# LoRA linear layer on one NeuronCore: a second buffer of rounded rows, a load cut in two, and another wait before the first store

## The chip, the cores and the metric

The kernel runs on one core of one Trainium2 chip. The metric is device time in microseconds (us); the median of three runs of the kernel before is 164.86 us (164.70 to 165.10). A core has a matrix engine (TensorE, PE in the profile; its weight loads are listed as PEld), VectorE (DVE), ScalarE (ACT), GpSimd (POOL) and SyncE (SP), which here only issues transfers. The engines run side by side and meet at semaphores. Data moves between HBM and on-chip memory (SBUF) through 16 DMA engines; matrix results are written to PSUM, from which DVE or ACT copy them out.

## The reference

```python
x: [16, 2048, 256] f32     W: [256, 256] f32
lora_A: [256, 16]   lora_B: [16, 256]   lora_E: [16]   scale: 1.0

x_flat = x.reshape(-1, 256)                     # 32768 rows
y = x_flat @ W
lora_out = ((x_flat @ lora_A) * lora_E) @ lora_B
return (y + scale * lora_out).reshape(16, 2048, 256)
```

x is 33.6 MB and the output is as large, both float32. The kernel folds the low-rank part into one matrix, weff = W + scale * A diag(E) B, in bfloat16, and then computes x_flat @ weff.

## The kernel before

**Rows and chunks.** The 32768 rows are cut into eight chunks, numbered 0 to 7. `PLAN` (line 10) gives their sizes in rows per partition: 16, 32, 48, 48, 16, 16, 48, 32, which makes 256 on each of 128 partitions. A chunk of 16 is a transfer of 2 MB, one of 48 is 6 MB. In SBUF a ring `xy` of 176 rows per partition holds both the rows loaded and, written over them, the results. Chunks 0 to 5 fill the ring exactly, so chunks 6 and 7 are loaded into places whose results have been stored before.

**SP's order** is written out by hand and sets the order of the one DMA queue. SP issues W, load 0, the three small loads (lines 122 to 124) and loads 1 to 5 (line 126) without a wait. Then, for each chunk, it waits until the chunk's results are in the ring (`s_rdy`, line 128) and issues its store (line 132). Two more waits stand in this loop: before the first store SP waits until load `LEAD - 2` = 4 has landed (line 131), and after store 2 (`AFTER`, line 15) it waits for stores 0 and 1, issues load 6, waits for store 2, and issues load 7 (lines 133 to 136).

**A group** is 16 rows of each partition (`G`); there are 16 groups. For each group:

- DVE rounds the rows to bfloat16 in one instruction, into the one buffer `xb` (line 177, a CAST in the profile). At a chunk's first group it waits for the chunk's load first; at chunk 4 (`PAUSE`) it also waits until store 2 has landed (line 175).
- PE transposes the 16 rows in two parts of eight (line 200, into `ps_xt`, two bfloat16 values travelling as one float32 word), and DVE copies each part to SBUF (`xt`, line 191).
- PE multiplies (line 208, 32 matmuls into `ps_y`, four rows at a time, two buffers), and ACT copies each four rows back to the ring (line 157). The last `LATE` = 6 of these 64 copies are made by DVE, after its last copy of transposes.

DVE executes its instructions strictly in the order of the program: cast of group g, the two copies of g, cast of g+1, and so on. PE runs a hardware loop over the 16 groups (line 227), waiting for `xb`, for `xt` and for a free `ps_y`. POOL passes a chunk's last `ps_y` buffer back to PE (line 164).

**Start-up.** weff is made once: PE transposes A (it waits for A's own semaphore, line 216), DVE multiplies by E (waits for E's), POOL rounds B (waits for B's), PE multiplies, DVE adds W.

The core's last wait is for stores 3 to 7 (line 237; the profile gives it the number 268).

Of the kernel before, what the change touches and what calls it, by code (L numbers as in the profile page):

```python
# [6 lines left out]

PLAN = [16, 32, 48, 48, 16, 16, 48, 32]  # L10

RING = 176

LEAD = 6
AFTER = {2: [6, 7]}

PAUSE = 4

G, S, Q = 16, 8, 4

LATE = 6


@with_exitstack
def kernel(
# [11 lines left out]
    P = 128  # L37
    FP32 = mybir.dt.float32
    BF16 = mybir.dt.bfloat16

    x_flat = x.flatten_outer_dims()
    out_flat = out.flatten_outer_dims()
    N, K = x_flat.shape
    M = out_flat.shape[1]
    R = lora_B.shape[0]
    KC = K // P
    CHUNKS = len(PLAN)
    assert K == M == KC * P and sum(PLAN) * P == N and all(b % G == 0 for b in PLAN)

    def sbuf(name, shape, dt):  # L50
        return ctx.enter_context(nc.sbuf_tensor(name, shape, dt))

    def psum(name, shape, dt):
        return ctx.enter_context(nc.psum_tensor(name, shape, dt))

    xy = sbuf("xy", [P, RING, K], FP32)
    xb = sbuf("xb", [P, G, K], BF16)

    xt = [sbuf(f"xt{s}", [P, S, P, KC], BF16) for s in range(2)]
    w_sb = sbuf("w_sb", [P, KC, M], FP32)  # L60
    a_sb = sbuf("a_sb", [P, KC, R], FP32)
    b_sb = sbuf("b_sb", [R, M], FP32)
    e_sb = sbuf("e_sb", [R, 1], FP32)
    b_bf = sbuf("b_bf", [R, M], BF16)
    ate = sbuf("ate", [R, KC, P], BF16)
    weff = sbuf("weff", [P, KC, M], BF16)
    ident = sbuf("ident", [P, P], FP32)

    ps_xt = [psum(f"ps_xt{s}", [P, S, P], FP32) for s in range(2)]
    ps_y = [psum(f"ps_y{s}", [P, Q, M], FP32) for s in range(2)]  # L70

    ps_at = ps_y[0][:R, 0, :].rearrange("r (c p) -> r c p", c=KC)
    ps_aeb = ps_y[1][:, :KC, :]

    sem = tc.alloc_semaphore
    s_w, s_a, s_b, s_e = sem("s_w"), sem("s_a"), sem("s_b"), sem("s_e")
    s_in = [sem(f"s_in{i}") for i in range(CHUNKS)]
    starts = [sum(PLAN[:i]) for i in range(CHUNKS)]
    places = [r % RING for r in starts]
    assert sum(PLAN[:LEAD]) <= RING and all(r + b <= RING for r, b in zip(places, PLAN))  # L80

    owners = {
        i: [j for j in range(LEAD) if places[j] < places[i] + PLAN[i] and places[i] < places[j] + PLAN[j]]
        for i in range(LEAD, CHUNKS)
# [5 lines left out]
    s_lora = sem("s_lora")  # L90
    s_lpe = sem("s_lpe")
    s_xb = sem("s_xb")
    s_t = sem("s_t")
    s_xt = sem("s_xt")
# [4 lines left out]
    def rows_of(flat, i):  # L99
        b, r0 = PLAN[i], starts[i] * P  # L100
        return flat[r0:r0 + b * P, :].rearrange("(p b) k -> p b k", b=b)

    def ring_of(i):
        return xy[:, places[i]:places[i] + PLAN[i], :]


    def pieces(rows):
        return [(i, r) for i, b in enumerate(PLAN) for r in range(0, b, rows)]

    def rows_at(i, r, rows):  # L110
        return xy[:, places[i] + r:places[i] + r + rows, :]

    with tc.tile_critical(sync_engine=mybir.EngineType.SP, no_gpsimd_drain=True):  # L113
        sp, pe, dve, act, pool = nc.sync, nc.tensor, nc.vector, nc.scalar, nc.gpsimd


        def load(i):
            sp.dma_start(out=ring_of(i), in_=rows_of(x_flat, i)).then_inc(s_in[i], 16)

        sp.dma_start(out=w_sb[:], in_=W.rearrange("(p c) m -> p c m", c=KC)).then_inc(s_w, 16)  # L120
        load(0)
        sp.dma_start(out=a_sb[:], in_=lora_A.rearrange("(p c) r -> p c r", c=KC)).then_inc(s_a, 16)
        sp.dma_start(out=b_sb[:], in_=lora_B).then_inc(s_b, 16)
        sp.dma_start(out=e_sb[:], in_=lora_E[:, None]).then_inc(s_e, 16)
        for i in range(1, LEAD):
            load(i)
        for i in range(CHUNKS):
            sp.wait_ge(s_rdy, i + 1)
            if i == 0:

                sp.wait_ge(s_in[LEAD - 2], 16)
            sp.dma_start(out=rows_of(out_flat, i), in_=ring_of(i)).then_inc(s_out[min(i, again)], 16)
            for later in AFTER.get(i, []):
                for j in owners[later]:
                    sp.wait_ge(s_out[j], 16)
                load(later)
        for i in range(len(s_out) - 1):
            sp.wait_ge(s_out[i], 16)


        pool.memset(ident[:], 0.0).then_inc(s_id, 1)  # L141
        pool.wait_ge(s_id, 1)
        pool.affine_select(  # L143
            out=ident[:], in_=ident[:], compare_op=mybir.AluOpType.not_equal, fill=1.0,
            base=0, pattern=[[-1, P]], channel_multiplier=1,
        ).then_inc(s_id, 1)
        pool.wait_ge(s_b, 16)
        pool.tensor_copy(out=b_bf[:], in_=b_sb[:]).then_inc(s_lora, 1)  # L148

        copies = pieces(Q)

        def y_of(q, engine, copy):
            i, r = copies[q]
            engine.wait_ge(s_p, q + 1)
            done = copy(out=rows_at(i, r, Q), in_=ps_y[q % 2][:])  # L157
            if r + Q == PLAN[i]:
                done.then_inc(s_rdy, 1)
            else:  # L160
                done.then_inc(s_y[q % 2], 1)

        for i in range(CHUNKS - 1):
            pool.wait_ge(s_rdy, i + 1).then_inc(s_y[((starts[i] + PLAN[i]) // Q - 1) % 2], 1)


        for q in range(len(copies) - LATE):
            y_of(q, act, act.copy)


        for g, (i, r) in enumerate(pieces(G)):
            if r == 0:
                dve.wait_ge(s_in[i], 16)
            if r == 0 and i == PAUSE:
                dve.wait_ge(s_out[again - 1], 16)

            dve.tensor_copy(out=xb[:], in_=rows_at(i, r, G)).then_inc(s_xb, 1)  # L177
            if g == 0:
                dve.wait_ge(s_e, 16)
                dve.wait_ge(s_lpe, 1)  # L180
                dve.tensor_scalar(  # L181
                    out=ate[:], in0=ps_at, scalar1=e_sb[:], scalar2=float(scale),
                    op0=mybir.AluOpType.mult, op1=mybir.AluOpType.mult,
                ).then_inc(s_lora, 1)
                dve.wait_ge(s_w, 16)
                dve.wait_ge(s_lpe, 2)
                dve.tensor_add(out=weff[:], in0=w_sb[:], in1=ps_aeb).then_inc(s_lora, 1)  # L187
            for k in range(g * G // S, (g + 1) * G // S):

                dve.wait_ge(s_t, k + 1)  # L190
                dve.tensor_copy(  # L191
                    out=xt[k % 2][:].rearrange("w j p c -> w j (p c)"), in_=ps_xt[k % 2][:].bitcast(BF16),
                ).then_inc(s_xt, 1)
        for q in range(len(copies) - LATE, len(copies)):
            y_of(q, dve, dve.tensor_copy)


        def transposes(k):
            for j in range(S):
                t = pe.transpose(ps_xt[k % 2][:, j, :], xb[:, k * S + j, :].bitcast(FP32), ident[:])  # L200
            t.then_inc(s_t, 1)

        def products(k):
            for h in range(S // Q):
                pe.wait_ge(s_y[h], 1).then_inc(s_y[h], -1)  # L205
                for j in range(Q):
                    for c in range(KC):
                        m = pe.matmul(  # L208
                            ps_y[h][:, j, :], xt[k % 2][:, h * Q + j, :, c], weff[:, c, :],
                            start=(c == 0), stop=(c == KC - 1),  # L210
                        )
                m.then_inc(s_p, 1)

        for h in range(2):
            pe.sem_inc(s_y[h], 1)
        pe.wait_ge(s_a, 16)
        pe.wait_ge(s_id, 2)
        for c in range(KC):
            t = pe.transpose(ps_at[:, c, :], a_sb[:, c, :], ident[:])  # L219
        t.then_inc(s_lpe, 1)  # L220
        pe.wait_ge(s_lora, 2)
        for c in range(KC):
            m = pe.matmul(ps_aeb[:, c, :], ate[:, c, :], b_bf[:], start=True, stop=True)  # L223
        m.then_inc(s_lpe, 1)

        pe.wait_ge(s_lora, 3)
        with pe.Fori(0, sum(PLAN) // G):
            pe.wait_ge(s_xb, 1).then_inc(s_xb, -1)  # L228
            for k in range(G // S):
                transposes(k)  # L230
            for k in range(G // S):
                pe.wait_ge(s_xt, 1).then_inc(s_xt, -1)
                products(k)


    with tc.tile_critical(sync_engine=mybir.EngineType.SP, no_gpsimd_drain=True):
# [36 lines left out]
```

## Time and profile before

| | |
|---|---|
| median of the runs | 164.86 us |
| the profiled execution, its own time | 165.35 us |
| its span in the profile | 163.6 us |
| moved by the DMA engines | 67.4 MB, 412 GB/s over the span |
| PE busy | 96.8 us (59%) |
| DVE busy | 81.7 us (50%) |
| ACT busy | 57.2 us (35%) |
| cast of a group on DVE (line 177) | 16 of 2287 ns |
| copy of eight transposed rows on DVE (line 191) | 32 of 1220 ns |
| copy of four result rows on ACT (line 157) | 58 of 1016 ns |
| first store issued | 53.03 us |
| store 2 landed, load 7 issued | 88.4 us |
| last store issued | 143.66 us |

Times inside the span count from its start. A transfer's landing is the time of its issue plus the time to landing that the profile gives for the issue. Because there is one queue, transfers follow each other, and the difference of two successive landings is what the later one took of the queue. In the rows for stretches of time, each engine's busy time comes with the number of its instructions, then the clock that PE was granted (1.00 is full speed), the mean busy share of the 16 DMA engines, and the rate. A packet is counted where it starts, so rates of short stretches scatter. The value behind "idle before" or in square brackets is how long an engine stood before an instruction, and what ended that.

### The profile page before, as it was taken

To read this page: it belongs to the slowest core of one execution; us is meant where nothing else is said; L and a number is where in the kernel's file an instruction comes from. 1 tells how busy PE (TensorE), PEld (TensorE's weight loads), DVE (VectorE), ACT (ScalarE), POOL (GpSimd) and SP (SyncE) were. 2 spreads that over 40 slices of the span, in tenths; PEclk is the share of its full clock that TensorE was granted. 3 is DMA by queue.
4 is the path that set the end of the run, shared out by engine and by line. 5 is a ranking of instruction groups with operands and counts; after the bars stand their busy time and mean duration, and the time that the engine had idled before them with its cause. 6 is when DMAs were issued, how large, how long until landed. Compare 5 with 4: busy or idle time off the path is not lost. (4 is left out here: it accounts for less than half of the span.)

```text
span 163.6 us, 1911 instructions
## 1 busy us (share of the span) xinstructions
PE 96.8 (59%) x772; PEld 79.3 (49%) x772; DVE 81.7 (50%) x56; ACT 57.2 (35%) x59; POOL 2.9 (2%) x7
## 2 busy tenths in 40 slices
PE   0027989877888978984000788878889775700000
PEld 0006677756777757763000767667777564500000
DVE  0063767559486494650003485594864949710000
ACT  3000357472664844747000054926648400000000
POOL 1050000000000000000000000000000000000000
PEclk9999999999999999999755599999999998775555
DMA  5999988998899999999999997999997999989990
GB/s 152 433 440 457 513 385 385 445 517 385 385 405 437 377 433 465 409 425 529 421 397 385 409 517 341 441 457 401 469 469 337 429 429 481 505 385 397 425 409 16
DMA packets 2658, 67.42 MB, mean 412 GB/s; under 512 B 464, under 2 KB 480, under 8 KB 608
## 3 DMA queue, kind: packets, MB, share of 16 engines
q1 hardware_dynamic: 2656, 67.41, 96.8%
q14 instruction: 2, 0.02, 0.0%
HBM read 33.85 MB, written 33.55 MB: 412 GB/s over the span
## 5 line engine op out<-in xcount | busy, mean ns | idle before, releaser
L157 ACT COPY xy<-ps_y 128x1024 f32<-128x1024 f32 x58 | 56.0, 1016 | 72.8 <-PE ps_y L208 72.8
L208 PE MATMUL ps_y<-weff,xt 128*128 128x256 bf16 x512 | 64.0, 278 | 16.9 <-PEq L205 16.8
L208 PEld LDWEIGHTS ps_y<-weff,xt 128*128 128x128 bf16 x512 | 48.0, 100 | 32.2 <-issue 24.4
L191 DVE COPY xt<-ps_xt 128x2048 bf16<-128x2048 bf16 x32 | 37.9, 1220 | 31.4 <-PE ps_xt L200 31.3
L177 DVE CAST xb<-xy 128x4096 bf16<-128x4096 f32 x16 | 36.6, 2287 | 28.6 <-DMA out_dram<-xy 16.0
L200 PE MATMUL ps_xt<-ident,xb 128*128 128x128 f32 x256 | 33.7, 290 | 17.3 <-PEq L228 17.3
L200 PEld LDWEIGHTS ps_xt<-ident,xb 128*128 128x128 f32 x256 | 31.1, 151 | 18.6 <-issue 18.5
L157 DVE COPY xy<-ps_y 128x1024 f32<-128x1024 f32 x6 | 7.2, 1220 | 1.2 <-PE ps_y L208 1.1
L219 PE MATMUL ps_y<-ident,a_sb 128*16 128x128 f32 x2 | 0.6, 402 | 9.3 <-DMA a_sb<-in_lora_A_dram 9.3
L219 PEld LDWEIGHTS ps_y<-ident,a_sb 128*16 128x16 f32 x2 | 0.1, 94 | 9.3 <-DMA a_sb<-in_lora_A_dram 9.3
L148 POOL CAST b_bf<-b_sb 16x256 bf16<-16x256 f32 x1 | 2.2, 2196 | 7.8 <-DMA b_sb<-in_lora_B_dram 7.8
L223 PE MATMUL ps_y<-b_bf,ate 16*128 16x256 bf16 x2 | 0.6, 404 | 2.0 <-DVE ate L181 2.0
L157 ACT ACT_TABLE_LOAD x1 | 1.3, 1283 | 0.9 <-SPq L113 0.9
L223 PEld LDWEIGHTS ps_y<-b_bf,ate 16*128 16x128 bf16 x2 | 0.1, 106 | 2.4 <-DVE ate L181 2.4
L187 DVE TENSOR_TENSOR weff<-w_sb,ps_y 128x512 bf16<-128x512 f32 x1 | 0.7, 689 | 0.8 <-PE ps_y L223 0.8
L181 DVE TENSOR_SCALAR ate<-ps_y,e_sb 16x256 bf16<-16x256 f32 x1 | 0.5, 466 | 0.0
L143 POOL TENSOR_SCALAR_AFFINE_SELECT ident<-ident 128x128 f32<-128x128 f32 x1 | 0.3, 294 | 0.2 <-POOL ident L141 0.2
L141 POOL MEMSET ident<- 128x128 f32 x1 | 0.2, 205 | 0.5 <-SPq L113 0.5
L254 POOL MEMSET const-float32-0.0<- 128x1 f32 x1 | 0.1, 100 | 0.2 <-issue 0.2
L254 POOL MEMSET const-bfloat16-1.0<- 128x1 bf16 x1 | 0.1, 103 | 0.0
L254 POOL MEMSET const-uint8-127<- 128x1 uint8 x1 | 0.1, 103 | 0.0
L254 POOL MEMSET const-float32-1.0<- 128x1 f32 x1 | 0.1, 100 | 0.0
## 6 DMA issues: line engine op xcount, KB each, us to landing
xy<-in_x_dram SPq DMA_DIRECT2D x3, 6144.0 KB, 29.9
out_dram<-xy SPq DMA_DIRECT2D x3, 6144.0 KB, 31.3
xy<-in_x_dram SPq DMA_DIRECT2D x2, 4096.0 KB, 20.1
out_dram<-xy SPq DMA_DIRECT2D x2, 4096.0 KB, 19.1
xy<-in_x_dram SPq DMA_DIRECT2D x3, 2048.0 KB, 48.2
out_dram<-xy SPq DMA_DIRECT2D x3, 2048.0 KB, 31.6
w_sb<-in_W_dram SPq DMA_DIRECT2D x1, 256.0 KB, 2.8
a_sb<-in_lora_A_dram SPq DMA_DIRECT2D x1, 16.0 KB, 7.4
```

The costliest lines, as they stand in the source:

```text
L143: pool.affine_select(out=ident[:], in_=ident[:], compare_op=mybir.AluOpType.not_equal, fill=1.0, base=0, pattern=[[-1, P]], channel_multip ...
L148: pool.tensor_copy(out=b_bf[:], in_=b_sb[:]).then_inc(s_lora, 1)
L157: done = copy(out=rows_at(i, r, Q), in_=ps_y[q % 2][:])
L177: dve.tensor_copy(out=xb[:], in_=rows_at(i, r, G)).then_inc(s_xb, 1)
L181: dve.tensor_scalar(out=ate[:], in0=ps_at, scalar1=e_sb[:], scalar2=float(scale), op0=mybir.AluOpType.mult, op1=mybir.AluOpType.mult,).the ...
L187: dve.tensor_add(out=weff[:], in0=w_sb[:], in1=ps_aeb).then_inc(s_lora, 1)
L191: dve.tensor_copy(out=xt[k % 2][:].rearrange("w j p c -> w j (p c)"), in_=ps_xt[k % 2][:].bitcast(BF16),).then_inc(s_xt, 1)
L200: t = pe.transpose(ps_xt[k % 2][:, j, :], xb[:, k * S + j, :].bitcast(FP32), ident[:])
L208: m = pe.matmul(ps_y[h][:, j, :], xt[k % 2][:, h * Q + j, :, c], weff[:, c, :], start=(c == 0), stop=(c == KC - 1),)
L219: t = pe.transpose(ps_at[:, c, :], a_sb[:, c, :], ident[:])
L223: m = pe.matmul(ps_aeb[:, c, :], ate[:, c, :], b_bf[:], start=True, stop=True)
L254: nc = _bacc.Bacc("TRN2", target_bir_lowering=False, num_devices=1)
```

## The change

Six edits go together.

1. `xb` becomes two buffers. PE's loop runs 8 times over two groups (one for each buffer) instead of 16 times over one.
2. DVE's order changes: the cast of group g+1 comes ahead of the two copies of group g (`early`) when g+1 is in the same chunk as g, or when it is the first of chunk 3, 5 or 7 (`EARLY`). At the first group of chunks 1, 2, 4 and 6 the cast stays behind those copies.
3. Load 5 (16 rows per partition) is issued as two transfers of 8 rows, each with its own semaphore (`LOADS`). DVE waits for both.
4. SP's wait before the first store is now for the first of these two instead of for load 4.
5. The last two entries of `PLAN` are exchanged: chunk 6 has 32 rows, chunk 7 has 48. Load 6 still needs the places of chunks 0 and 1, load 7 those of chunks 1 and 2. `LATE` goes from 6 to 5, so that ACT makes one copy more and DVE one fewer at the end.
6. The three small loads share one semaphore `s_l`; PE, POOL and DVE wait for all three (48) instead of each for its own.

```diff
-PLAN = [16, 32, 48, 48, 16, 16, 48, 32]
+PLAN = [16, 32, 48, 48, 16, 16, 32, 48]
+LOADS = {5: 2}
+EARLY = (3, 5, 7)
-LATE = 6
+LATE = 5
...
-    xb = sbuf("xb", [P, G, K], BF16)
+    xb = [sbuf(f"xb{s}", [P, G, K], BF16) for s in range(2)]
...
         def load(i):
-            sp.dma_start(out=ring_of(i), in_=rows_of(x_flat, i)).then_inc(s_in[i], 16)
+            b = PLAN[i] // len(s_in[i])
+            for j, landed in enumerate(s_in[i]):
+                sp.dma_start(
+                    out=ring_of(i)[:, j * b:(j + 1) * b, :], in_=rows_of(x_flat, i)[:, j * b:(j + 1) * b, :],
+                ).then_inc(landed, 16)
...
             if i == 0:
-                sp.wait_ge(s_in[LEAD - 2], 16)
+                sp.wait_ge(s_in[LEAD - 1][0], 16)
...
-        pool.wait_ge(s_b, 16)
+        pool.wait_ge(s_l, 48)
...
-        for g, (i, r) in enumerate(pieces(G)):
+        rounds = pieces(G)
+        def round_rows(g):
+            i, r = rounds[g]
             if r == 0:
-                dve.wait_ge(s_in[i], 16)
+                for landed in s_in[i]:
+                    dve.wait_ge(landed, 16)
             if r == 0 and i == PAUSE:
                 dve.wait_ge(s_out[again - 1], 16)
-            dve.tensor_copy(out=xb[:], in_=rows_at(i, r, G)).then_inc(s_xb, 1)
+            dve.tensor_copy(out=xb[g % 2][:], in_=rows_at(i, r, G)).then_inc(s_xb, 1)
+        def early(g):
+            return g < len(rounds) and (rounds[g][1] > 0 or rounds[g][0] in EARLY)
+        round_rows(0)
...
+        for g in range(len(rounds)):
+            if early(g + 1):
+                round_rows(g + 1)
             for k in range(g * G // S, (g + 1) * G // S):
                 dve.wait_ge(s_t, k + 1)
                 dve.tensor_copy(
                     out=xt[k % 2][:].rearrange("w j p c -> w j (p c)"), in_=ps_xt[k % 2][:].bitcast(BF16),
                 ).then_inc(s_xt, 1)
+            if g + 1 < len(rounds) and not early(g + 1):
+                round_rows(g + 1)
...
-        with pe.Fori(0, sum(PLAN) // G):
-            pe.wait_ge(s_xb, 1).then_inc(s_xb, -1)
-            for k in range(G // S):
-                transposes(k)
-            for k in range(G // S):
-                pe.wait_ge(s_xt, 1).then_inc(s_xt, -1)
-                products(k)
+        with pe.Fori(0, sum(PLAN) // G // 2):
+            for g in range(2):
+                pe.wait_ge(s_xb, 1).then_inc(s_xb, -1)
+                for k in range(G // S):
+                    transposes(g, k)
+                for k in range(G // S):
+                    pe.wait_ge(s_xt, 1).then_inc(s_xt, -1)
+                    products(k)
```

More of the change, by code (lines that the diff above doesn't have):

```diff
@@ L75 @@
     sem = tc.alloc_semaphore
-    s_w, s_a, s_b, s_e = sem("s_w"), sem("s_a"), sem("s_b"), sem("s_e")
-    s_in = [sem(f"s_in{i}") for i in range(CHUNKS)]
+    s_w = sem("s_w")
+    s_l = sem("s_l")
+    s_in = [[sem(f"s_in{i}_{j}") for j in range(LOADS.get(i, 1))] for i in range(CHUNKS)]
     starts = [sum(PLAN[:i]) for i in range(CHUNKS)]
@@ L117, in load @@
         def load(i):
-            sp.dma_start(out=ring_of(i), in_=rows_of(x_flat, i)).then_inc(s_in[i], 16)
+            b = PLAN[i] // len(s_in[i])
[3 more added lines that the diff above has]
+                ).then_inc(landed, 16)
         sp.dma_start(out=w_sb[:], in_=W.rearrange("(p c) m -> p c m", c=KC)).then_inc(s_w, 16)
         load(0)
-        sp.dma_start(out=a_sb[:], in_=lora_A.rearrange("(p c) r -> p c r", c=KC)).then_inc(s_a, 16)
-        sp.dma_start(out=b_sb[:], in_=lora_B).then_inc(s_b, 16)
-        sp.dma_start(out=e_sb[:], in_=lora_E[:, None]).then_inc(s_e, 16)
+        sp.dma_start(out=a_sb[:], in_=lora_A.rearrange("(p c) r -> p c r", c=KC)).then_inc(s_l, 16)
+        sp.dma_start(out=b_sb[:], in_=lora_B).then_inc(s_l, 16)
+        sp.dma_start(out=e_sb[:], in_=lora_E[:, None]).then_inc(s_l, 16)
         for i in range(1, LEAD):
@@ L168 @@
             y_of(q, act, act.copy)
-        for g, (i, r) in enumerate(pieces(G)):
+        rounds = pieces(G)
+        def round_rows(g):
+            i, r = rounds[g]
             if r == 0:
-                dve.wait_ge(s_in[i], 16)
+                for landed in s_in[i]:
+                    dve.wait_ge(landed, 16)
             if r == 0 and i == PAUSE:
                 dve.wait_ge(s_out[again - 1], 16)
-            dve.tensor_copy(out=xb[:], in_=rows_at(i, r, G)).then_inc(s_xb, 1)
[L178 to L187, printed above, removed]
+            dve.tensor_copy(out=xb[g % 2][:], in_=rows_at(i, r, G)).then_inc(s_xb, 1)
+        def early(g):
+            return g < len(rounds) and (rounds[g][1] > 0 or rounds[g][0] in EARLY)
+        round_rows(0)
+        dve.wait_ge(s_l, 48)
+        dve.wait_ge(s_lpe, 1)
+        dve.tensor_scalar(
+            out=ate[:], in0=ps_at, scalar1=e_sb[:], scalar2=float(scale),
+            op0=mybir.AluOpType.mult, op1=mybir.AluOpType.mult,
+        ).then_inc(s_lora, 1)
+        dve.wait_ge(s_w, 16)
+        dve.wait_ge(s_lpe, 2)
+        dve.tensor_add(out=weff[:], in0=w_sb[:], in1=ps_aeb).then_inc(s_lora, 1)
+        for g in range(len(rounds)):
+            if early(g + 1):
+                round_rows(g + 1)
             for k in range(g * G // S, (g + 1) * G // S):
@@ L193, with transposes @@
                 ).then_inc(s_xt, 1)
+            if g + 1 < len(rounds) and not early(g + 1):
+                round_rows(g + 1)
         for q in range(len(copies) - LATE, len(copies)):
             y_of(q, dve, dve.tensor_copy)
-        def transposes(k):
+        def transposes(g, k):
             for j in range(S):
-                t = pe.transpose(ps_xt[k % 2][:, j, :], xb[:, k * S + j, :].bitcast(FP32), ident[:])
+                t = pe.transpose(ps_xt[k % 2][:, j, :], xb[g][:, k * S + j, :].bitcast(FP32), ident[:])
             t.then_inc(s_t, 1)
@@ L215 @@
             pe.sem_inc(s_y[h], 1)
-        pe.wait_ge(s_a, 16)
+        pe.wait_ge(s_l, 48)
         pe.wait_ge(s_id, 2)
```

## The prediction

> **What bounds the kernel now.** I read the page's slices and queue table first, then what SyncE (SP) waited for, then the landings of single transfers around the first store, then the compute engines.
>
> ```profile
> DMA  5999988998899999999999997999997999989990
> q1 hardware_dynamic: 2656, 67.41, 96.8%
> HBM read 33.85 MB, written 33.55 MB: 412 GB/s over the span
> ```
>
> One queue keeps the 16 DMA engines busy for 96.8% of the span. TensorE (PE) is busy 59%, VectorE (DVE) 50%, ScalarE (ACT) 35%. So an edit counts only where it empties or slows this queue.
>
> ```profile
> SPq L131 <- DMA xy<-in_x_dram: 47.2, 1, 47.2
> SPq L268 <- DMA out_dram<-xy: 17.5, 1, 17.5
> ```
>
> The first store is held 47.2 us by a load, not by compute, and after the last issue the core only waits 17.5 us for data. The chain of waits stops at that last store and names 2% of PE and 1% of DVE. Next come single issues: loads 4 and 5 (counted from 0), stores 0 and 5; in each, start and length of the issue, or us from issue to landing.
>
> ```profile
> 4.70 0.49 SPq L118 DMA_DIRECT2D xy<-in_x_dram  x1
> xy<-in_x_dram SPq DMA_DIRECT2D x1, 2048.0 KB, 48.2
> 5.23 0.49 SPq L118 DMA_DIRECT2D xy<-in_x_dram  x1
> xy<-in_x_dram SPq DMA_DIRECT2D x1, 2048.0 KB, 52.9
> 53.03 4.39 SPq L132 DMA_DIRECT2D out_dram<-xy  x3
> out_dram<-xy SPq DMA_DIRECT2D x1, 2048.0 KB, 10.0
> out_dram<-xy SPq DMA_DIRECT2D x1, 2048.0 KB, 31.6
> ```
>
> Load 4 lands at 4.70+48.2 = 52.9, load 5 at 58.1, store 0 at 63.0. Load 3 (issue 4.22, 43.8 to landing) lands at 48.0. The steps between equal 16-row transfers are thus 4.9, 5.2 and 4.9 us: load 5, the one after whose predecessor the first store is issued, loses 0.3 us. The rate by stretches says the same (us; then PE, PEld, DVE, ACT, POOL; granted clock, DMA share, GB/s):
>
> ```profile
> 50.40:52.80 2.40, 1.72 (x16) 1.41 (x15) 2.40 (x3) 0.05 (x1) 0.00 (x0) 1.00 1.03 437
> 52.80:55.20 2.40, 2.08 (x20) 1.53 (x19) 2.07 (x1) 2.00 (x3) 0.00 (x0) 1.00 1.00 423
> 55.20:57.60 2.40, 2.40 (x24) 2.26 (x21) 0.68 (x1) 1.86 (x2) 0.00 (x0) 1.00 0.99 348
> 57.60:60.00 2.40, 1.71 (x17) 1.43 (x16) 2.40 (x3) 0.48 (x1) 0.00 (x0) 1.00 1.02 437
> ```
>
> 348 against about 430 GB/s for 2.4 us is (430-348)/430 x 2.4 = 0.46 us, with the engines still counted busy (0.99): transfers slow down where the queue passes from loads to stores; it does not run empty.
>
> **The change, part by part.** The sum is made against the profiled execution (165.35 us: span 163.6, 1.75 around it); its median of runs is 164.86, 0.49 lower, and I add the change to that median.
>
> *Load 5 in two transfers.* One more issue on SP, 0.49 us at about 5.7; its data is due at 53, so 47 us hide it. On the queue: a 16-row step is 4.9 us and a 48-row step 14.5 (load 2 to load 3, 33.5 to 48.0), so 32 rows cost 9.6, 16 rows 4.8, and a transfer itself about 0.1 (the unrounded steps, 4.89 and 14.53, give 0.07). I take +0.07; ends 0 and +0.1. The Trainium skill, "DMA: Bandwidth & Descriptors", section on the anatomy of one DMA, speaks against the split: it fits 2.0 us plus bytes over 436 GB/s to one transfer (issued from GpSimd), so by it a second piece would add 2.0 us and the sum would be about +1.7; the rows show that such a cost is not paid between transfers that queue behind each other, and nothing else here uses that figure.
>
> *The first store's wait* moves from load 4 to the first half of load 5. Eight rows are half of 4.9, so it ends at about 52.9+2.5 = 55.4 and store 0 is issued near 55.5 instead of 53.03. Queued behind it on SP: store 1 (ready long before, 53.43 becomes 55.9), store 2 (57.09, waits for ACT anyway), and the waits for loads 6 and 7, which end on landed stores (73.17, 88.38). What remains of load 5 to cover the start of store 0 is 2.5 us less the time between last data and landing. The launch of an idle queue is seen at the very start:
>
> ```profile
> 0.95 0.38 SPq L120 DMA_DIRECT2D w_sb<-in_W_dram  x1
> 1.50:1.95 0.45, 0.00 (x0) 0.00 (x0) 0.00 (x0) 0.45 (x1) 0.17 (x1) 1.00 0.00 0
> 1.95:2.40 0.45, 0.00 (x0) 0.00 (x0) 0.00 (x0) 0.24 (x1) 0.00 (x0) 1.00 1.18 86
> ```
>
> Nothing moves until 1.0 us after the issue; all 256 KB of W land 2.8 us after it, 0.6 us of which is data at 430 GB/s, so latency is between 1.0 and 2.2 us. With 0.1 us for SP to wake, store data flows 1.1 to 2.3 us after the first half landed, against 2.5 us less a landing lag that cannot be over the 1.2 between those two ends: from 1.4 us of slack to 1.0 us of gap. I take no gap, since the middles (1.7 and 1.9) leave a little slack. In exchange the two kinds of transfer overlap less: the 0.3 us that load 5 lost can be saved, between 0 (the loss belongs to the change of direction) and 0.46 (the rate's figure). I take 0.33 (5.21-4.88, unrounded), because landings are what the next transfer follows. Ends for this part: -0.46 and +1.0.
>
> *Chunks 6 and 7 change sizes (48, 32 to 32, 48).* The bytes are the same. Load 6 still waits for store 1 (73.17), load 7 for store 2 (88.38); behind load 7's issue the queue then holds load 6, 9.7 us instead of 14.7, far above the launch. Load 6 lands near 98 instead of 103.1, load 7 at 112.8 as before. Cost 0.
>
> *Rounding ahead.* The 16 casts (2287 ns) and 32 copies (1220 ns) stay. In the steady rhythm this changes nothing: PE goes from a group's products straight into the next transposes, so the cast was never late.
>
> ```profile
> 60.67 1.95 PE L208 MATMUL ps_y<-weff,xt 128*128 128x256 bf16 x16 [0.32 <-PEq L205]
> 62.46 1.91 PE L200 MATMUL ps_xt<-ident,xb 128*128 128x128 f32 x16
> ```
>
> A wait is added where a chunk's first cast comes ahead of the last copies of the chunk before: chunks 3, 5 and 7. For 3 (landed 48.0) and 5 (58.1) the data is there. For 7 it is not: DVE stands until load 7 lands, 112.8, casts to 115.1, and only then makes the two copies of chunk 6's last group, whose transposes were ready at 113.2:
>
> ```profile
> 113.23 2.36 DVE L191 COPY xt<-ps_xt 128x2048 bf16<-128x2048 bf16 x2 [2.05 <-PE ps_xt L200]
> 135.33 3.66 DVE L157 COPY xy<-ps_y 128x1024 f32<-128x1024 f32 x3
> 143.66 0.33 SPq L132 DMA_DIRECT2D out_dram<-xy  x1
> ```
>
> Queued behind: PE's products of that group, then all three groups of chunk 7. Everything from there runs 1.9 us late. One of the six final copies goes to ACT (LATE 5), which takes about 1.2 us off DVE's end, so the last store is issued between 144.4 (143.66+1.9-1.2) and 145.6. The queue is then fed by store 6: store 5 lands at 106.26+31.6 = 137.9, and 32 rows more end at 147.6; before, 48 rows ended at 152.6. The cover shrinks from 8.9 us to 2.0 to 3.2, against 1.0 to 2.2 for a launch. Cost 0, with little to spare.
>
> *Start-up.* PE and POOL now wait for all three small loads (e_sb lands at 2.81+6.8 = 9.6) instead of a_sb (PE 9.33) and b_sb (POOL 9.50): 0.1 to 0.3 us later on the first group. Cover: chunk 0 is wanted at 53.
>
> *PE's loop* has twice the body, 8 passes. The Trainium skill, "Runtime: NRT & Kernel Launch", section on instruction fetch mechanics, says that a taken branch out of the fetched window stalls for a fetch; the instruction queue of this trace moved 2 packets in the whole span, and whether the longer body fetches again no run here shows. Cost 0.
>
> Sum: +0.07 - 0.33 = -0.26 us, 164.86-0.26 = 164.6.
>
> **The rivals.** A measurement of this kernel can tell about 0.2% (0.33 us) from no change.
>
> (a) Slower, *the queue runs dry before store 0*. Place: 56 to 58 us. If the launch takes the long end and the landing lag is long, up to 1.0 us is lost, +0.07 for the split. It decides once store 0's data comes later than the last packet of load 5. For it: W's 2.8 us. Against: 1.0 us to the first movement. 165.2 to 165.9; the middle, a gap of 0.5, gives 165.4.
>
> (b) Slower, *the last store comes late*. The granted clock of PE went to 0.5 after stretches in which PE stood (80 to 92 us, and 0.75 on average over 136 to 140). The stall at 113 could trigger this: 16 matmuls take 62.46-60.67 = 1.8 us in the rows above, and as much again at half clock. 145.6+1.8 = 147.4 plus a launch of 1.0 to 2.2 passes 147.6 by 0.8 to 2.0, less 0.26 of gain: 165.4 to 166.6. Against: the lower estimate, 144.4+1.0, is 2.2 us early.
>
> (c) *Nothing moves*: the 0.3 us belongs to the change from loads to stores whatever the issue time. 164.9. For it: the next change, from store 2 to load 6, shows 393 GB/s from 86 to 92 us although load 6 had been queued for 13 us.
>
> (d) *More is saved*: the rate's 0.46 us, and something of that second dip (0.5 us), since load 6 now has another size. 164.1 to 164.5.
>
> **How the numbers follow.** Forecast 0.49 (centre 164.6; about half of it saves over 0.33 through the rate's figure), (a) 0.16, (b) 0.12, (c) 0.13, (d) 0.10. Faster: 0.24+0.10 = 0.34. Same: 0.25 of the forecast, 0.10 of (c), 0.03 from the light ends of (a) and (b) = 0.38. Slower: 0.14+0.11+0.03 = 0.28. For the range, (d) below 164.1 is left out, and of (a) and (b) what passes 165.5, together under 2 in 10; the forecast's own range is 164.3 to 164.9.
>
> **What would show it.** Right: SP's wait at the first store ends near 55.4; the step from load 4's landing to the second half of load 5 is 5.0 us or less, and the stretch from 55 to 60 us shows no rate below 400. Casts: two in a row at chunk starts 3, 5 and 7. The last copies of chunk 6 begin near 115.1, the last store is issued between 144 and 146, and the core's last wait is about 14.5 + 2 us. Wrong: a stretch after 56 us with the DMA share clearly under 0.9 (a), a DMA share that falls in the slices after 145 us (b), idle time of PE at each turn of its loop (a fetch), or landings of later stores that move by more than the first store's does.

## The result, and the profile after

The changed kernel takes 165.88 us (median of 6 runs, 165.72 to 166.06) against 164.78 us for the kernel before (6 runs): ratio 1.0068, interval 1.0055 to 1.0082. It is 1.1 us slower. The forecast was 164.6 us, range 164.1 to 165.5.

The page of the changed kernel, slices and queue table:

```profile
DMA  4999988998999999999997998996988999999990
...
q1 hardware_dynamic: 2800, 67.41, 96.9%
q8 instruction: 1, 0.02, 0.0%
q14 instruction: 2, 0.02, 0.0%
```

The queue is as full as before (96.9%), the bytes are the same, the span is 164.1 us. One line is new: a queue q8 that moved one packet of instructions (before, q14 was the only instruction queue). The profiled execution of before (165.35 us) lies 0.6 us above its median, this one (165.89) at its median, so the spans show less of the difference than the times do.

Load 2 of the kernel before, its issue and its us to landing:

```profile
3.73 0.45 SPq L118 DMA_DIRECT2D xy<-in_x_dram  x1
xy<-in_x_dram SPq DMA_DIRECT2D x1, 6144.0 KB, 29.8
```

The same for the changed kernel: loads 2 and 4, the two halves of load 5, the issue of store 0, loads 6 and 7:

```profile
3.75 0.45 SPq L125 DMA_DIRECT2D xy<-in_x_dram  x1
xy<-in_x_dram SPq DMA_DIRECT2D x1, 6144.0 KB, 31.3
4.72 0.43 SPq L125 DMA_DIRECT2D xy<-in_x_dram  x1
xy<-in_x_dram SPq DMA_DIRECT2D x1, 2048.0 KB, 49.6
5.19 0.44 SPq L125 DMA_DIRECT2D xy<-in_x_dram  x1
xy<-in_x_dram SPq DMA_DIRECT2D x1, 1024.0 KB, 51.6
5.67 0.44 SPq L125 DMA_DIRECT2D xy<-in_x_dram  x1
xy<-in_x_dram SPq DMA_DIRECT2D x1, 1024.0 KB, 53.6
56.88 0.35 SPq L141 DMA_DIRECT2D out_dram<-xy  x1
73.88 0.34 SPq L125 DMA_DIRECT2D xy<-in_x_dram  x1
xy<-in_x_dram SPq DMA_DIRECT2D x1, 4096.0 KB, 24.3
88.52 0.34 SPq L125 DMA_DIRECT2D xy<-in_x_dram  x1
xy<-in_x_dram SPq DMA_DIRECT2D x1, 6144.0 KB, 25.1
```

Load 2 lands at 35.0, where it landed at 33.5 before: 1.5 us are lost long before the first store. The loads behind it land late by about as much (load 4 at 54.3 instead of 52.9, the first half of load 5 at 56.8 instead of the 55.4 forecast). Load 7 lands 15.4 us after load 6 (98.2 to 113.6), for 48 rows that took 14.5 elsewhere.

The stretches around the first store (granted clock, DMA share and GB/s are the last three numbers):

```profile
55.20:57.60 2.40, 2.08 (x20) 1.54 (x18) 2.04 (x1) 2.03 (x3) 0.00 (x0) 1.00 0.80 335
57.60:60.00 2.40, 2.40 (x24) 2.23 (x21) 0.71 (x1) 1.83 (x2) 0.00 (x0) 1.00 1.03 433
```

The share falls to 0.80 (0.2 of 2.4 us, about 0.5 us): here engines are idle, where before they were slow but busy (0.99). The compute side, DVE's casts and copies around load 7's landing and the last store's issue:

```profile
113.68 2.29 DVE L191 CAST xb<-xy 128x4096 bf16<-128x4096 f32 x1 [4.50 <-DMA xy<-in_x_dram]
115.89 2.35 DVE L212 COPY xt<-ps_xt 128x2048 bf16<-128x2048 bf16 x2
...
144.10 0.33 SPq L141 DMA_DIRECT2D out_dram<-xy  x1
```

DVE stands 4.5 us for load 7 with the copies of chunk 6's last group behind it, and the last store is issued at 144.1. The forecast had 144.4 to 145.6. It is harmless: the store ahead of it lands only between 147.1 and 148.3.

**Sixteen landings for one transfer.** The semaphore of a transfer is raised 16 times, and the trace holds these 16 times; I take them for one landing on each of the 16 DMA engines. Their distances hardly change from one transfer to the next (loads 1 to 4 of before: 0.73, 0.73, 0.73 and 0.72 us between the first and the last), so an engine that has fallen behind seems to stay behind. The transfer has landed when the last of the 16 has. I therefore use two numbers per transfer, computed from these times: the *spread* between the first and the last, and the *loss*. The loss is the step of the mean landing from the transfer before, less what the step should be: 0.065 us and 0.3014 us per row (from loads 3 and 4 of before, 14.53 us for 48 rows and 4.89 for 16). Load 5 counts as one transfer even where it is issued in pieces, so each further piece adds its own 0.065 us to the loss. All runs, one profiled execution of each, in us (time is the median of the runs):

```
run            time   spread   loss at    loss at    loss at   loss at   last store lands
               median load 2   load 5+    store 1    store 2+  load 7    first / mean / last
                               store 0               load 6
before         164.8   0.73     0.34       0.0        0.45      0.04    159.7 160.3 162.3
after          165.9   2.11     0.60       0.0        0.75      0.98    161.6 162.0 162.8
e1_swap        164.7   0.64     0.41       0.0       -0.05      0.06    159.4 160.0 161.5
e2_gate        165.4   0.44     0.08       0.0        0.20      0.57    160.0 160.5 161.8
e3_ahead       165.8   2.05     0.02       0.0        0.05      0.24    159.3 160.0 162.5
e4_unswap      165.6   1.59     0.29       0.0        0.75      0.99    161.2 161.7 162.5
e5_loop2       166.0   1.66     0.01       0.0       -0.03      0.48    159.3 160.2 162.8
e6_loop4       165.6   2.18     0.01       0.0        0.05      0.44    159.4 160.1 162.5
e7_split       164.9   0.61     0.36       0.0        0.03      0.02    159.5 159.9 161.5
e8_late        166.9   0.77     1.90       0.0        0.80      0.93    162.7 163.2 163.9
e9_half        169.6   0.76     3.24       0.0        0.86      0.81    163.0 164.4 166.4
e10_all        170.2   0.70     4.45       0.0        0.46      1.01    164.6 165.6 167.1
e11_quarter    165.3   0.57     0.29       0.0       -0.03      0.35    159.4 160.1 162.2
e12_nowait     165.0   0.38     0.31       0.0        0.02      0.24    159.5 160.1 162.1
e13_dry        167.1   0.43     0.17       1.85       0.82      0.96    163.0 163.5 164.1
e14_oldwait    165.9   1.81     0.00       0.0       -0.02      0.36    161.1 161.4 162.8
```

In e9_half and e10_all the first loss holds the extra store as well.

**One packet takes an engine's place.** In all six runs with the packet on q8 (after, e3, e4, e5, e6, e14) 16 data packets are under way at almost every moment of the 3 us before it, and 15 while it runs (1.01 to 1.08 us). The data packet of 48 KB that starts as it ends takes 2.31 us, the others around it 1.82 (at most 1.88). So one DMA engine loses about 1.5 us here. At load 1, ahead of the packet, the spread is 0.5 to 0.8 us in these runs, no more than in the others; at load 2 it is 1.6 to 2.2, against 0.4 to 0.8 in the ten runs without the packet.

### The profile page after: what moved, and what is told of

Its sections match the earlier page's. It is cut to its first block, busy times and chain, and to the rows that moved or that the text cites. A ratio compares the mean times of both kernels' runs of the same rounds, so it can differ in the third digit from the quotient of the medians.

```text
span 164.1 us, 1898 instructions
## 1 busy us (share of the span) xinstructions
PE 95.6 (58%) x772; PEld 78.5 (48%) x772; DVE 80.1 (49%) x55; ACT 58.2 (35%) x60; POOL 2.6 (2%) x7
## 3 DMA queue, kind: packets, MB, share of 16 engines
q1 hardware_dynamic: 2800, 67.41, 96.9%
## 5 line engine op out<-in xcount | busy, mean ns | idle before, releaser
L166 ACT COPY xy<-ps_y 128x1024 f32<-128x1024 f32 x59 | 57.0, 1015 | 75.8 <-PE ps_y L231 75.8
L231 PE MATMUL ps_y<-weff,xt 128*128 128x256 bf16 x512 | 62.6, 274 | 20.1 <-PEq L228 20.0
L231 PEld LDWEIGHTS ps_y<-weff,xt 128*128 128x128 bf16 x512 | 46.9, 98 | 35.1 <-issue 28.0
L166 DVE COPY xy<-ps_y 128x1024 f32<-128x1024 f32 x5 | 5.9, 1218 | 0.2
## 6 DMA issues: line engine op xcount, KB each, us to landing
xy<-in_x_dram SPq DMA_DIRECT2D x3, 6144.0 KB, 31.3
```

The costliest lines, as they stand in the source:

```text
L231: m = pe.matmul(ps_y[h][:, j, :], xt[k % 2][:, h * Q + j, :, c], weff[:, c, :], start=(c == 0), stop=(c == KC - 1),)
```

## The experiments

Three theories on which edit costs the time: S (the exchange of sizes), G (the first store's wait), A (rounding ahead with PE's longer loop). One run for the edits of each theory, and one for the change without the exchange.

**e1_swap**

```diff
-PLAN = [16, 32, 48, 48, 16, 16, 48, 32]
+PLAN = [16, 32, 48, 48, 16, 16, 32, 48]
```

> Kernel before with the last two chunk sizes exchanged (32, 48) and nothing else. Theory S (the exchange: load 7, now 48 rows, loses about 1 us where the queue turns from loads to stores): 0.8 to 1.1 us slower than before, ratio 1.005 to 1.007, and load 7 takes about 15.5 us of the queue instead of 14.5. Theory G (the later first store leaves the engines idle at 57 us): no difference, within 0.3 us. Theory A (rounding ahead, with the longer loop of PE): no difference, within 0.3 us.

Measured: 164.73 against 164.90, ratio 0.9994 (0.9981 to 1.0008). Load 7 loses 0.06 us. Theory S falls, although the changed kernel does lose 0.98 us at load 7.

**e2_gate**

```diff
+LOADS = {5: 2}
...
-                sp.wait_ge(s_in[LEAD - 2], 16)
+                sp.wait_ge(s_in[LEAD - 1][0], 16)
```

> Kernel before with load 5 in two transfers and the first store behind the first of them, nothing else. Theory G: 0.5 to 1.0 us slower, ratio 1.003 to 1.006, and store 0 takes 5.4 us of the queue instead of 4.9. Theory S: within 0.3 us of before. Theory A: within 0.3 us of before.

Measured: 165.44 against 164.90, ratio 1.0041 (1.0021 to 1.0061): in size theory G. But in the profiled execution nothing runs dry. Issue of store 0, then the stretch where it starts:

```profile
55.56 0.35 SPq L138 DMA_DIRECT2D out_dram<-xy  x1
```

```profile
55.20:57.60 2.40, 2.40 (x24) 2.27 (x22) 0.66 (x1) 1.88 (x2) 0.00 (x0) 1.00 1.05 440
```

Issue at 55.56 and 440 GB/s where it was 348: the predicted saving is there (loss 0.08 instead of 0.34, 0.06 of the 0.08 for the second piece). It is given back at load 7 (0.57 instead of 0.04): the four losses add up to 0.85 us here and to 0.83 in the profile of before. This execution took 164.90 us, the fastest of its eight and no slower than the median of before. What makes the median 0.5 us longer this trace therefore doesn't show; that the queue runs dry in other executions is not excluded.

**e3_ahead**

```diff
 (changed kernel)
-PLAN = [16, 32, 48, 48, 16, 16, 32, 48]
+PLAN = [16, 32, 48, 48, 16, 16, 48, 32]
-LOADS = {5: 2}
+LOADS = {}
-LATE = 5
+LATE = 6
-                sp.wait_ge(s_in[LEAD - 1][0], 16)
+                sp.wait_ge(s_in[LEAD - 2][0], 16)
```

> Changed kernel with the sizes, LATE, the single load 5 and the first store's wait as before: what is left of the change is the two buffers, the rounding ahead, PE's longer loop and the shared semaphore of the small loads. Theory A: 0.6 to 1.1 us slower, with one DMA engine held up by a fetch of instructions near 33 us. Theories S and G: within 0.3 us of before.

Measured: 165.82 against 164.90, ratio 1.0066 (1.0049 to 1.0082), with the packet on q8 and a spread of 2.05 us at load 2. This part alone is as slow as the whole change (1.0068).

**e4_unswap**

```diff
 (changed kernel)
-PLAN = [16, 32, 48, 48, 16, 16, 32, 48]
+PLAN = [16, 32, 48, 48, 16, 16, 48, 32]
```

> Changed kernel with the chunk sizes of before (48, 32). Theory S: the loss is gone, within 0.3 us of before. Theory G: 0.5 to 1.0 us slower than before. Theory A: 0.6 to 1.1 us slower than before.

Measured: 165.58, ratio 1.0047 (1.0031 to 1.0064). The loss at load 7 stays (0.99) without the exchange. The queue falls to a DMA share of 0.92 from 55 to 58 us, so it too has a short gap. The losses of e2_gate and e3_ahead (0.5 and 0.9 us) do not add up: this run, which has both parts, is 0.7 us slower.

Is it DVE's new order, or the length of PE's loop?

**e5_loop2**

```diff
-        with pe.Fori(0, sum(PLAN) // G):
-            pe.wait_ge(s_xb, 1).then_inc(s_xb, -1)
-            ...
+        with pe.Fori(0, sum(PLAN) // G // 2):
+            for _ in range(2):
+                pe.wait_ge(s_xb, 1).then_inc(s_xb, -1)
+                ...
```

> Kernel before with PE's loop written as 8 passes over two groups; one buffer, DVE's order, sizes and first store as before. Theory F (the longer program of PE makes its instruction queue fetch 16 KB while the data queue is full, and the one DMA engine that carries it stays about 1.4 us behind, so that every later landing waits for it): one more packet on an instruction queue near 33 us, the spread of load 2's landings over the 16 engines goes from 0.7 to about 2 us, and the time is 0.7 to 1.0 us longer (ratio 1.004 to 1.006). Theory A' (DVE's new order costs it): no difference, within 0.3 us.

Measured: 166.03 against 164.73, ratio 1.0080 (1.0065 to 1.0096), with one buffer and the order of before. The queue table, and load 2:

```profile
q1 hardware_dynamic: 2656, 67.41, 96.2%
q8 instruction: 1, 0.02, 0.0%
```

```profile
3.73 0.45 SPq L118 DMA_DIRECT2D xy<-in_x_dram  x1
xy<-in_x_dram SPq DMA_DIRECT2D x1, 6144.0 KB, 31.0
```

Load 2 lands at 34.7 instead of 33.5. The packet is of 16,384 bytes and starts at 30.9 us (32.9 in the changed kernel); it takes 1.07 us. The records do not name the engine of a packet, but from load 2 on one landing of the 16 stands behind the others. Theory F holds: the longer loop alone brings the packet, the lag and the loss of time. The time is longer than the 0.7 to 1.0 us expected, and the spread smaller (1.66 instead of about 2). Compute is not what ends late: the last store is issued at 144.3, while the store ahead of it lands from 149.6 on.

The lag is not simply carried to the end. In e3, e5 and e6 the last landing is 1.3 to 1.8 us behind the mean at load 2 and 1.5 to 2.0 at load 6, loses another 0.7 to 1.1 us at load 7, where a second landing also falls back, and ends 2.5 to 2.7 us behind. In the runs with neither packet nor gap (before, e1, e2, e7, e11, e12) the last landing ends 1.3 to 2.2 us behind the mean too, most of it lost after 90 us. The means hardly differ (160.0 to 160.2 against 159.9 to 160.5). Why more is lost at load 7 after the packet, no run shows.

**e6_loop4**

```diff
+        with pe.Fori(0, sum(PLAN) // G // 4):
+            for _ in range(4):
```

> As the last, with 4 passes over four groups. Theory F: the program of PE grows by about 13 KB more, so at least one more fetch of 16 KB, or one in every pass if the body no longer stays fetched: 1.5 to 3 us slower than before if the same DMA engine carries them, about 0.8 if they fall on different ones. Theory A': no difference, within 0.3 us.

Measured: 165.63, ratio 1.0057 (1.0044 to 1.0071). Still one packet, at 31.3 us, and load 2 lands 1.4 us late once: the loop's body is not fetched again in each pass, and a body twice as long again brings no second fetch. The expected further fetch did not come; the 0.9 us are those of one fetch.

**e7_split**

```diff
 (e2_gate)
-                sp.wait_ge(s_in[LEAD - 1][0], 16)
+                sp.wait_ge(s_in[LEAD - 2][0], 16)
```

> Kernel before with load 5 in two transfers, the first store still behind load 4. Both theories of the first store's wait (G: the queue runs dry at the turn; L: engines that are lined up at the first store all turn from stores to loads and back at the same moment, and lose up to 1 us at the turns near 87 and 110 us) expect the split alone to cost 0 to 0.1 us; a loss of 0.5 us here would put it on the split.

Measured: 164.90 against 164.73, ratio 1.0012 (0.9992 to 1.0032). The second transfer costs next to nothing, so what e2_gate loses beyond that is put on the wait (the two intervals overlap slightly).

**e8_late**

```diff
-                sp.wait_ge(s_in[LEAD - 2], 16)
+                sp.wait_ge(s_in[LEAD - 1], 16)
```

> Kernel before with the first store behind the whole load 5, in one transfer. Theory G (only the gap at the first store counts): the store is issued at 58.3, its data starts about 1 us later, a gap of 1.3 to 1.7 us less the 0.3 us that load 5 loses today: 1.0 to 1.4 us slower. Theory L: the same and, because all engines start store 0 together, 0.3 us more at the turn from store 2 to load 6 and 0.9 us more at the turn from load 7 to store 3: 2.0 to 2.7 us slower.

Measured: 166.85, ratio 1.0128 (1.0111 to 1.0144). The stretches where the queue stands empty:

```profile
55.00:58.00 3.00, 2.90 (x27) 2.49 (x24) 0.95 (x2) 1.93 (x2) 0.00 (x0) 1.00 0.62 262
58.00:61.00 3.00, 2.10 (x18) 1.70 (x19) 3.00 (x3) 1.35 (x2) 0.00 (x0) 1.00 0.84 350
```

The gap costs 1.9 us, and the later turns (store 2 to load 6, load 7 to store 3) lose 0.80 and 0.93 us, theory L's sizes. The launch can be read here: the last data of load 5 end at 57.5, it lands at 58.0, the store is issued at 58.06, and its first data packet starts at 58.9. The last engine suffers less than the mean (+1.6 against +2.8 us beside the profile of before): engines that lag catch up in the gap (the spread at store 0 is 0.20 us, at load 5 it was 0.76), and the final spread falls from 2.6 to 1.15 us.

**e9_half** and **e10_all** (n is 8 or 16; the extra store writes input rows to a scratch tensor and changes nothing else)

```diff
-                sp.wait_ge(s_in[LEAD - 2], 16)
+                sp.wait_ge(s_in[LEAD - 1], 16)
+                sp.dma_start(out=pad[:n], in_=ring_of(4)[:n]).then_inc(s_pad, 16)
```

> Kernel before with the first store behind the whole load 5 (as in the run with the late store, 166.85 us), and ahead of that store an extra store of 8 partitions of chunk 4's input (16 KB each, into a scratch tensor that nothing reads), which occupies 8 of the 16 DMA engines for 0.6 us. Theory L (engines that start store 0 together lose most at the later turns): the two halves are 0.6 us apart, the turn from store 2 to load 6 loses 0.45 instead of 0.8 us, the one from load 7 to store 3 at most 0.4 instead of 0.9; 0 to 0.6 us faster than the run with the late store, 166.2 to 166.8. Rival (the later turns lose because the whole queue is later, or for another reason): turns as in that run, and 0.3 to 0.6 us slower than it, 167.1 to 167.4.

> The same with an extra store of 16 partitions, which occupies all 16 engines for 0.6 us and leaves them lined up. Both theories: 0.6 us slower than the run with the late store, 167.3 to 167.5; theory L: turns that lose 0.7 to 0.8 and 0.9 us as there, so that this run is 0.5 to 1.2 us slower than the one with half the engines, though the data added differs by 128 KB only.

Measured: 169.58 (ratio 1.0291, 1.0267 to 1.0315) and 170.24 (1.0325, 1.0301 to 1.0349). Both expectations missed: the extra store cost 2.7 and 3.4 us instead of 0.6, and set the two halves 2 us apart instead of 0.6. In the trace the first 8 and 16 packets behind its issue take 2.3 to 3.1 us each, where 16 KB take 0.61 elsewhere; why is open. Still the test speaks: with the halves 2 us apart the turns lose 0.86 and 0.81 us, as much as with engines lined up in e8_late (0.80 and 0.93), and with all 16 engines occupied 0.46 and 1.01. Theory L falls.

**e11_quarter** and **e12_nowait**

```diff
 (e2_gate)
-LOADS = {5: 2}
+LOADS = {5: 4}
```

```diff
-            if i == 0:
-                sp.wait_ge(s_in[LEAD - 2], 16)
```

> Kernel before with load 5 in four transfers of 4 rows and the first store behind the first of them (landed near 54.2 us). Theory P (a store that is issued far ahead of its turn slows the last loads, one that is issued after the queue is nearly dry lines the engines up; between them there is a better moment): load 5 loses under 0.15 instead of 0.34 us, later turns as before, 0.1 to 0.4 us faster than before. Theory M (each later issue costs more): 0.1 to 0.3 us slower than before.

> Kernel before without the wait of SP for a load ahead of the first store, which is then issued near 23 us, behind 35 us of queued loads. Theory P: load 5 loses as much as before or more, 0 to 0.4 us slower. Rival (the loss at load 5 comes from the issue itself, 4 us ahead of its turn; load 7, whose following store was queued 24 us ahead, lost 0.04 us): load 5 loses nothing, 0.2 to 0.4 us faster.

Measured: 165.29 (ratio 1.0021, 1.0004 to 1.0037) and 164.98 (0.9996, 0.9977 to 1.0014). With no wait load 5 loses the same 0.31 us, so the loss is not made by the issue four us ahead of its turn, and the wait of before buys nothing that these runs can tell. With the wait at a quarter load 5 loses 0.29 us, 0.20 of which are its three further pieces; the rest is under theory P's 0.15, but load 7 loses 0.35, and the time is 0.45 us longer, not shorter: towards theory M. No moment was found that beats the kernel before.

What is left is that later turns cost more once the queue has run dry.

**e13_dry**

```diff
             sp.wait_ge(s_rdy, i + 1)
+            if i == 1:
+                sp.wait_ge(s_out[0], 16)
```

> Kernel before, with SP waiting for the landing of store 0 before it issues store 1, so that the queue runs dry once between two stores (63 us) and not at the turn from loads to stores. Theory D (once the queue has run dry, the two later turns cost more, whatever the place): store 1 takes about 1.9 us more of the queue, then load 7 takes 10.5 us or more instead of 9.7 and stores 2 and load 6 together 0.7 us more than their packets; 2.3 to 3 us slower than before. Theory C (only a dry first turn does that): later turns lose 0 to 0.4 us in all; 1.2 to 2.0 us slower.

Measured: 167.11 against 164.89, ratio 1.0141 (1.0119 to 1.0163). The stretch with the gap, and load 7:

```profile
61.00:64.00 3.00, 3.00 (x30) 2.74 (x28) 0.94 (x2) 2.46 (x3) 0.00 (x0) 1.00 0.37 158
```

```profile
89.93 0.34 SPq L118 DMA_DIRECT2D xy<-in_x_dram  x1
xy<-in_x_dram SPq DMA_DIRECT2D x1, 4096.0 KB, 25.4
```

Load 7 lands 10.9 us after load 6 (104.4 to 115.3), instead of 9.7, though the gap was between two stores, 50 us earlier, and the first turn was the usual one. In size of the turns' losses this is theory D; the time, 2.2 us slower, falls just short of its 2.3 (the interval of the ratio is 2.0 to 2.7 us); the final spread shrank here too, to 1.1 us. All six runs with a gap (after, e4, e8, e9, e10, e13) lose 0.81 to 1.01 us at load 7, the other ten 0.02 to 0.57, each in one profiled execution.

**e14_oldwait**

```diff
 (changed kernel)
-LOADS = {5: 2}
+LOADS = {}
-                sp.wait_ge(s_in[LEAD - 1][0], 16)
+                sp.wait_ge(s_in[LEAD - 2][0], 16)
```

> Changed kernel with load 5 in one transfer and the first store behind load 4, as before; two buffers, rounding ahead, sizes 32 and 48 and LATE 5 stay. Theory F (the fetch of instructions explains the whole loss, the late first store adds a gap but lets the lagging engine catch up): as slow as the changed kernel, 0.8 to 1.2 us slower than before, last landings spread by 3 us over the engines. Rival (the two losses add up): 0.4 to 0.7 us faster than the changed kernel, 165.2 to 165.5.

Measured: 165.86 against 164.89, ratio 1.0059 (1.0041 to 1.0078): as slow as the changed kernel, 165.88. With everything else in place the first store's wait costs nothing more. The last store here lands between 161.1 and 162.8, in the changed kernel between 161.6 and 162.8: the wait moves the mean, not the last engine. The last landing is the same by two ways. In the changed kernel the gap lets the lagging engine catch up (0.4 us behind the mean at store 2, 0.8 at the end), and all engines are late. Here the lag grows to 2.8 us.

## Why the prediction was wrong, point by point

- *What bounds the kernel*: right. Every run follows the DMA queue, and the compute edits here matter by what they do to that queue. But the reading by one landing per transfer and by the mean share of 16 engines hid what counts, the last of the 16.
- *"PE's loop has twice the body, 8 passes ... Cost 0"*: this step failed. The term was put at nothing though the prediction said that no run shows it, and by itself it is enough for the whole loss. e5_loop2 shows +1.3 us for the longer loop alone (ratio 1.0080), e3_ahead +0.9 us with two buffers and rounding ahead, the change +1.1. I looked for the cost on PE, as idle time at the turns of the loop; it lies on one DMA engine, which loses about 1.5 us when 16 KB of instructions are fetched with the data queue full, and load 2 lands 0.9 to 1.5 us later. The Trainium skill, "Runtime: NRT & Kernel Launch", section on instruction fetch mechanics, has instructions fetched in blocks of 16 KiB, which is the size of the packet seen, and calls the crossing of a block mostly hidden. Here it is hidden from PE, whose pauses around the packet in e5_loop2 are 0.69 and 0.32 us as before, and not from the data. Where in the program the fetch is triggered no run shows, and no run has the two buffers without the longer loop.
- *"The first store's wait": -0.33, ends -0.46 and +1.0*: this step failed too. Its first half was right: alone (e2_gate) the issue came at 55.56 for a forecast 55.5, no gap opened in the profiled execution, and load 5's loss went from 0.34 to 0.08 us. But that did not shorten the time, which rose by 0.5 us, within my upper end; in the profiled execution the 0.3 us were lost again at load 7, which the step held unchanged, and the 0.5 us are open. The same saving also comes without the edit: in e3, e5, e6 and e14, which keep the old wait, the late landing of load 4 moves the issue to 54.2 to 54.6, and load 5 and store 0 lose 0.02 us or less. In the changed kernel the lag of the fetch delayed the wait's end to 56.8, so the engines that were not behind ran dry for 0.5 us; that gap cost the mean 0.5 us (0.34 were lost there before) and the later turns another 0.3 and 0.9, and gave the lagging engine time to catch up. Net, by e14_oldwait against the change: 0.
- *Rival (a), the queue runs dry before store 0, 165.2 to 165.9*: its place and its sign (a DMA share of 0.80) came, and the time lies in its range. That the time fits is luck: for a gap of 0.5 us its own sum gives 165.4, the gap came from the fetch's lag and not from a long launch (0.9 us from the issue to the first data in e8_late, for 1.0 to 2.2 assumed), and e14_oldwait is as slow without the gap.
- *Split, +0.07*: right (e7_split, 1.0012 with 1 inside the interval; in e2_gate the two pieces take 4.96 us for 4.89). The fixed 2.0 us that the Trainium skill, "DMA: Bandwidth & Descriptors", section on the anatomy of one DMA, fits to one transfer issued from GpSimd are not paid between these queued transfers.
- *Sizes exchanged, 0*: right by e1_swap. *Rounding ahead, 0 with little to spare*: the stall came as worked out (copies at 115.9 for 115.1), the last store's issue a little early (144.1 for 144.4 to 145.6). PE's granted clock stayed at 1.00 from 112 to 144 us, so rival b did not occur in the changed kernel. In e14_oldwait the last store was issued at 145.3 and most engines waited for it (first landing 161.1 instead of 159.3 in e3_ahead), while the slowest did not: the cover was as thin as said. There the granted clock did fall behind the stall (0.60 from 116 to 120 us), as rival b had it.
- *Start-up*: hidden, as said. PE began 0.5 us later (9.86 for 9.33) where 0.1 to 0.3 were forecast, the first transposes under 0.1 later.

What stays open: why turns of the queue cost 0.8 to 1.0 us after it has once run dry. Lined-up engines do not explain it. The two go together whether the queue runs dry at the first turn (e8_late) or between two stores (e13_dry), but no run shows by what way. Open too is the 0.5 us of e2_gate.

## What to carry to other kernels

When one DMA queue is full from end to end, count everything that shares its 16 engines, instruction fetches among them: here a loop body of two groups instead of one cost 0.9 to 1.3 us, and the page shows its fetch in one line of the queue table. Look at the landings of all 16 engines, not at one landing or a mean: the time is that of the engine that ends last. And do not wait with the next issue until the queue runs dry: in e8_late the gap cost 1.9 us at its place, and two later turns lost 0.8 and 0.9.

## What the runs showed of the hardware that was not expected

- One instruction fetch of 16 KB took the place of a data packet on one DMA engine for 1.01 to 1.08 us, more than the 0.61 us that 16 KB of data take, and the data packet behind it took 2.31 instead of 1.82 us (six of six runs). The spread of load 2's landings went from 0.4 to 0.8 us to 1.6 to 2.2.
- A queue that had run dry once, whether between loads and stores or between two stores, lost 0.8 to 1.0 us at the turn from loads to stores 50 us later (six of six runs; 0.02 to 0.57 in the ten others). Why is open.
- A store of 128 or 256 KB issued into an empty queue, ahead of the first large store, cost 2.7 and 3.4 us; the first 8 and 16 packets of 16 KB behind its issue took 2.3 to 3.1 us each.
- Two transfers of 1 MB in a row took little more than one of 2 MB (4.96 against 4.89 us).
